# A planner's chains without a gap, four more pairs by seven products, and h and the fourth output chunk handled in another order

## The chip, the cores and the metric

The kernel runs on one core of one Trainium2 chip. The metric is the device time of one execution in microseconds (us), lower is better. The kernel before takes 1148.96 us, the median of 3 runs (1148.46 to 1150.25).

## The reference

One layer of a hybrid encoder on 256 tokens of width 2048, in 32-bit floats. Cut to what matters:

```python
hn = rms_norm(h, g_mix_pre)                       # (256, 2048)
u = hn @ w_in                                     # 2048 x 5120: q, k, v, x, gate
attn = neighborhood_attention(q, k, v, rpb)       # 8 heads of 128
rec = rglru_bidirectional(x, ...) * gelu(gate)    # width 1024
mixed = concat(rms_norm(attn, g_attn_out), rms_norm(rec, g_rec_out)) @ w_out   # 2048 x 2048
h = h + rms_norm(mixed, g_mix_post)
fn = rms_norm(h, g_ffn_pre)
ff = (silu(fn @ w_ffn_gate) * (fn @ w_ffn_up)) @ w_ffn_down    # 2048 x 5632 twice, 5632 x 2048
h = h + rms_norm(ff, g_ffn_post)
gate = sigmoid(rms_norm(h, g_ple_pre) @ w_ple_gate)            # 2048 x 2048
h = h + rms_norm(gate * (p @ w_ple_proj), g_ple_post)          # p is (256, 256)
```

## The kernel before, in words

**Products.** The tokens are two tiles of 128. Every product is done in three matmuls, because both sides are split in a high part that the matmul takes as it is and a low part, the rest: high by high, high by low, low by high (`products`, L565 to L567; `times3`, L577 to L579). A matmul is 128 x 128 by 128 x 512. The weights come from memory as tiles of 128 x 2 x 512 (512 KB, two blocks of 128 rows each, a pair "k") into a few raw slots `wr` (`load_stream`, L491, all on SP's queue). ACT casts a tile to its high part `wh` (`hi_stream`, L516), DVE subtracts it to get the low part `wl` (`lo_stream`, L526). There are 6 slots for the split tiles, one more from the FFN on, and one more that is lent.

**Seven products in place of eight.** The FFN's gate and up projection, the down projection and the last gate work on a pair of output chunks by a `Group`. For each pair k of row blocks a unit is either plain ("p": 8 block products, 24 matmuls) or by the Strassen-Winograd scheme ("s": 7 block products, 21 matmuls, `seven`). An "s" unit needs sums of weight blocks (`sum_stream`: four subtractions of 128 x 512 on DVE, L546 and L550, into slots `ts`), and its second raw tile is split by half only: the first tile, half the second and the two sums are split, three and a half tiles in place of two. It needs sums of activation blocks too (`act_sums`, L1574 and the split of L312 and L314, once per pair k and left side). The matmuls of "s" units that have no plain partner gather in four banks p1, p5, p6 and p7; after the last "s" unit of a group, `Seven.early` (L1695 to L1708) combines them, and `late` adds the result to the other four banks. Which units are "s" is written by hand: `KINDS` (L89) has one digit for each of the 11 groups of gate and up, "2" or "3" being their number (group 0 uses `FIRST` with two), and `DOWN` (L66) lists the units of the down projection by part. Part 3 has one group for chunks 0 and 1, and plain chunks 2 and 3 after it.

**From the gate to the down projection.** `Gated.late` multiplies gate and up, turns the blocks (a DVE transpose, and a round trip through memory by DMA, `turn`, L348 and L356) and splits them into `mid0`, `mid1` or `mid2`, the left side of the down projection of the three parts: groups 0 to 3, 4 to 7 and 8 to 10. Where the down projection has an "s" unit, `act_sums` follows.

**The mixing layer's output.** `w_out` has four chunks of 512 columns, each with an attention half (`A_KS`, four pairs) and a recurrent half (`R_KS`). They have different scales per token (`r_attn` and `r_rec`, the reciprocals of roots `rt_attn` and `rt_rec`), so for each chunk `attn_part` (L1625) writes the attention half times `r_attn` to `mg` on ACT, and `rec_part` (L1639) adds the recurrent half times `r_rec` on DVE. Then `summed` takes the sum of squares (`squares`, L1423, ACT) and multiplies by the gain (L1415, DVE). The order is attention 0, attention 1, recurrent 0, recurrent 1, then attention and recurrent of 2, and of 3. Then PE has two chunks of the small embedding product while `next_norm` sums the squares (L1438), takes the root, waits for all four chunks' gains, and computes h (L1459), which PE transposes (L332) and ACT and DVE split (L318, L320) as the left side of the FFN.

**Lending.** h is needed again only after the FFN. When the squares of h (L1470) are planned, `lend_h` writes h to memory (L1483, `kept`, 2 x 1024 KB), and its two buffers serve as one split slot (`lent_w`) and two raw slots (`lent_r`) until `give_back` loads h again. The gain's buffer is lent as the two slots for sums (`lent_t`).

**The order of the work.** The kernel builds its instruction queues with a `Plan` that runs while the program is written. Each task is a generator that yields its next operation's engine and cost: DVE 0.08 + 0.00104 us per element, ACT 0.12 + 0.00082, a matmul 0.2267. The plan keeps a clock per engine, starts the task with the earliest start plus its due time ("late": URGENT, SOON, LATE, ...), and writes its instructions at that place of the queues. After an operation the task is ready again 0.15 us (`SEM`) after its end. PE's products are in fixed order; transposes and other small matmuls go between them when the plan holds them ready. Nothing of the plan's time is on the chip: each engine runs its queue in order and waits by semaphores.

Of the kernel before, what the change touches and what calls it, by code (L numbers as in the profile page):

```python
# [10 lines left out]
F32 = mybir.dt.float32  # L11
# [5 lines left out]
P = 128  # L17
# [41 lines left out]
SM_BUFS = 4  # L59
LATE = 0.6  # L60
MM = 0.2267
# [3 lines left out]
TURN_LATE = -6.0  # L65
DOWN = (("p2 p6 s0 p8 p10 s4 s12 p14", "p2 p6 s0 p10 s4 p8 s12 p14"), ("p2 p6 s0 p8 p10 s4 s12 p14", "p2 p6 s0 p10 s4 p8 s12 p14"), ("p2 p4 s0 p6 p8 p10",))  # L66
URGENT = -3.0
SOON = -0.5
TURNS = 1
# [14 lines left out]
LATE_SUMS = 0.0  # L84
SEED = 0.0
LATE_EVAC = 0.0
# [21 lines left out]
class Plan:  # L108
# [10 lines left out]
    LATENCY = 2.0  # L119
    MARGIN = 0.4  # L120

    def __init__(self, **slots):
# [129 lines left out]
def layer(ctx: ExitStack, tc: tile.TileContext, a: dict, out: bass.AP):  # L252
# [772 lines left out]

    r_of = {n: const.tile([P, NT], F32, name=f"r_{n}") for n in ("attn", "rec")}
    ev_r = {n: Event() for n in r_of}

    def token_rstd(ss, n):
# [7 lines left out]
        tmp = const.tile([P, NT], F32, name=f"rt_{n}")  # L1037
        yield act(NT, SQRT, give="sm")
# [250 lines left out]
    def open_p2():  # L1289
        for e in mixT.ev + list(ev_r.values()):  # L1290
            plan.reach(e)
        p1_ctx.close()
        rs = ctx.enter_context(tc.tile_pool(name="rs", bufs=1))
        t2["pool"] = rs
        t2["mg"] = rs.tile([P, NT, D], F32, name="mg")
# [59 lines left out]
    class Sub:  # L1355


        def __init__(self, name, gain, gname):
# [7 lines left out]
        def chunk(self, c, ch, add=False):  # L1366
# [7 lines left out]
            for t in range(NT):  # L1374
# [5 lines left out]
                plan.add(self.squares(c, t, src, squared[t]), plan.now, URGENT if c == 3 else 0.0)  # L1380
            for t in range(NT):
                src = mg[:, t, sl] if add else ch.accs[t]
                if early:
                    yield act(N)
                    nc.scalar.copy(mg[:, t, sl], src)
                else:
                    if add:
                        yield squared[t]
                    yield dve(N)
                    nc.vector.tensor_tensor(  # L1390
                        out=mg[:, t, sl], in0=src, in1=t2["gain"][:, sl], op=ALU.mult
                    )
            for e in squared:
# [26 lines left out]
        def squares(self, c, t, src, ev):  # L1420
            yield act(N)
            junk = t2["pool"].tile([P, N], F32, tag="junk", name="junk", bufs=1)
            nc.scalar.activation(junk, src, AF.Square, accum_out=self.ss[:, t, c : c + 1])  # L1423
            done(ev)
            done(self.sums[c][t])
# [4 lines left out]
    def next_norm(sub, nxt, rstd, ev_rstd, g_next):  # L1430
# [171 lines left out]

    mix = Sub("mix", "g_mix_post", "g_ffn_pre")
    hF = Act()
    rstd_f, ev_rf = small("rstd_f"), Event()
# [489 lines left out]
```

## Time and profile before

| | |
|---|---|
| median of 3 runs | 1148.96 us |
| the profiled execution | 1149.72 us, span 1147.9 us |
| PE busy, matmuls | 1134.6 us, 5135 |
| DVE busy | 973.4 us |
| ACT busy | 722.5 us |
| DMA | 257.69 MB, mean 224 GB/s |
| granted TensorE clock | 0.998 |

PE is the matmul engine (PEld its weight loads), DVE the vector engine, ACT the scalar engine, SP the one whose queue issues nearly all DMAs. A row of waits reads: who waited, at which line, for whom; total us, times, longest. A row of a window has its length, then busy us and the number of instructions of PE, PEld, DVE, ACT and POOL, the granted clock, the DMA engines' busy share and GB/s. A row of a timeline has the start, the duration, the engine, the line, the operation, out<-in, the shapes and a count; in brackets how long the engine sat idle before it and what ended that. Durations of neighbours overlap, so the cost of one among many is read from start to start. A matmul of 512 columns shows 0.39 us and starts 0.227 us after the one before.

### The profile page before, as it was taken

How to read it: one execution, taken by the hardware profiler on the slowest of the kernel's cores; microseconds unless marked ns; L12 is line 12 of the kernel's file. 1: busy time of each engine (PE TensorE's matmuls, PEld its weight loads, DVE VectorE, ACT ScalarE, POOL GpSimd, SP SyncE). 2: the span in 40 equal slices, each digit the busy share in tenths (PEclk: the TensorE clock that was granted, in tenths of full speed). 3: DMA queues.
4: the chain of work that ended last, by engine and by line, in shares of the span. 5: the costliest groups of instructions: out<-in, count | busy, mean ns of one | idle time of the engine just before them, and what ended most of it. 6: DMA issues, size and time to landing. Idle time of an engine off the chain costs nothing.

```text
span 1147.9 us, 14639 instructions
## 1 busy us (share of the span) xinstructions
PE 1134.6 (99%) x5135; PEld 941.4 (82%) x5135; DVE 973.4 (85%) x1280; ACT 722.5 (63%) x975; POOL 1.6 (0%) x13
## 2 busy tenths in 40 slices
PE   9999999999999999999999999999999999999996
PEld 7888888888888788888888888888888888888885
DVE  6777887877659899889989889999987999877996
ACT  7775888686558755555565455565655547566863
POOL 0000000000000000000000000000000000000000
PEclk9999999999999999999999999999999999999999
DMA  9876768557865778586576776767776757985561
GB/s 354 290 241 203 251 194 240 167 181 261 321 196 174 256 242 264 197 254 227 194 235 195 222 218 187 224 231 214 223 244 202 220 186 245 295 305 185 173 194 73
DMA packets 83594, 257.69 MB, mean 224 GB/s; under 512 B 9024, under 2 KB 24768, under 8 KB 82112
## 3 DMA queue, kind: packets, MB, share of 16 engines
q1 hardware_dynamic: 83376, 256.68, 69.5%
q8 instruction: 40, 0.66, 0.2%
q14 instruction: 34, 0.28, 0.1%
q10 hardware_dynamic: 144, 0.08, 0.0%
HBM read 242.04 MB, written 14.68 MB: 224 GB/s over the span
## 4 chain that ended last, share of the span: by engine, by line
PE 96%; DMA 1%; ACT 1%; DVE 1%; issue 0%; SPq 0%; DVEq 0%; ACTq 0%
PE c L566 14%; PE c L567 14%; PE c L565 14%; PE acc L565 12%; PE acc L566 11%; PE acc L567 11%; PE p L579 3%; PE p L578 3%; PE p L577 3%; PE c L579 2%; PE c L578 2%; PE c L577 2%; DMA kept<-h 1%; PE tr L332 0%; DVE h L1459 0%; ACT junk L1470 0%
## 5 line engine op out<-in xcount | busy, mean ns | idle before, releaser
L526 DVE TENSOR_TENSOR wl<-wr,wh 128x1024 fp32r<-128x1024 f32 (+1 forms) x318 | 368.6, 1171 | 78.3 <-ACT wh L516 77.0
L516 ACT CAST wh<-wr 128x1024 fp32r<-128x1024 f32 (+1 forms) x318 | 317.5, 1011 | 153.4 <-PE c L567 55.5
L565 PE MATMUL c<-wh,hT_mix_hi 128*128 128x512 f32 x428 | 167.0, 390 | 0.6 <-ACT hT_mix_hi L318 0.6
L567 PE MATMUL c<-wh,hT_mix_lo 128*128 128x512 f32 x428 | 166.6, 389 | 0.0
L566 PE MATMUL c<-wl,hT_mix_hi 128*128 128x512 f32 x428 | 166.5, 389 | 0.0
L516 ACT CAST wh<-lent_t 128x1024 fp32r<-128x1024 f32 x71 | 74.1, 1053 | 111.2 <-DVE lent_t L550 76.1
L565 PE MATMUL acc<-wh,hT_hi 128*128 128x512 f32 x320 | 126.5, 395 | 1.2 <-ACT wh L516 1.2
L566 PE MATMUL acc<-wl,hT_hi 128*128 128x512 f32 x320 | 125.3, 392 | 0.0
L567 PE MATMUL acc<-wh,hT_lo 128*128 128x512 f32 x320 | 125.2, 391 | 0.0
L565 PEld LDWEIGHTS c<-wh,hT_mix_hi 128*128 128x128 f32 x428 | 80.3, 188 | 17.4 <-ACT hT_mix_hi L318 0.9
L567 PEld LDWEIGHTS c<-wh,hT_mix_lo 128*128 128x128 f32 x428 | 80.3, 188 | 16.9 <-DVE hT_mix_lo L320 0.2
L566 PEld LDWEIGHTS c<-wl,hT_mix_hi 128*128 128x128 f32 x428 | 80.4, 188 | 16.5
L526 DVE TENSOR_TENSOR wl<-lent_t,wh 128x1024 fp32r<-128x1024 f32 x71 | 85.1, 1220 | 9.5 <-ACT wh L516 9.3
L516 ACT CAST wh<-lent_r 128x1024 fp32r<-128x1024 f32 (+1 forms) x59 | 57.4, 986 | 29.1 <-PE c L567 20.1
L565 PEld LDWEIGHTS acc<-wh,hT_hi 128*128 128x128 f32 x320 | 60.5, 189 | 13.2 <-ACT wh L516 1.5
L567 PEld LDWEIGHTS acc<-wh,hT_lo 128*128 128x128 f32 x320 | 60.4, 189 | 12.8
L566 PEld LDWEIGHTS acc<-wl,hT_hi 128*128 128x128 f32 x320 | 60.5, 189 | 12.4 <-DVE wl L526 0.4
L526 DVE TENSOR_TENSOR wl<-lent_r,wh 128x1024 fp32r<-128x1024 f32 (+1 forms) x59 | 66.7, 1136 | 3.0 <-ACT wh L516 3.0
L578 PE MATMUL p<-wl,sums_f 128*128 128x512 f32 x75 | 29.3, 390 | 0.0
L579 PE MATMUL p<-wh,sums_f 128*128 128x512 f32 x75 | 29.2, 389 | 0.0
L577 PE MATMUL p<-wh,sums_f 128*128 128x512 f32 x75 | 29.2, 389 | 0.0
L516 ACT CAST lent_w<-wr 128x1024 fp32r<-128x1024 f32 (+1 forms) x23 | 21.1, 916 | 11.0 <-PE c L567 10.0
(508 smaller groups left out, 2335.4 us busy)
## 6 DMA issues: line engine op xcount, KB each, us to landing
wr<-in_w_in SPq DMA_DIRECT2D x77, 512.0 KB, 4.7
wr<-in_w_ffn_down SPq DMA_DIRECT2D x70, 512.0 KB, 4.8
wr<-in_w_ffn_gate SPq DMA_DIRECT2D x64, 512.0 KB, 4.5
wr<-in_w_ffn_up SPq DMA_DIRECT2D x64, 512.0 KB, 4.3
wr<-in_w_out SPq DMA_DIRECT2D x32, 512.0 KB, 4.7
lent_r<-in_w_ffn_up SPq DMA_DIRECT2D x24, 512.0 KB, 4.2
lent_r<-in_w_ffn_gate SPq DMA_DIRECT2D x24, 512.0 KB, 4.3
wr<-in_w_ple_gate SPq DMA_DIRECT2D x24, 512.0 KB, 4.2
```

What stands on the lines that cost most here:

```text
L516: nc.scalar.copy(his[i][:, j, :], raws[i][:, j, :])
L526: nc.vector.tensor_tensor(out=los[i][:, j, :], in0=raws[i][:, j, :], in1=f32(his[i][:, j, :]), op=ALU.subtract,)
L565: nc.tensor.matmul(accs[t], hi[t], wh[:, j, :], start=st, stop=False, **mm)
L566: nc.tensor.matmul(accs[t], hi[t], wl[:, j, :], start=False, stop=False, **mm)
L567: nc.tensor.matmul(accs[t], lo[t], wh[:, j, :], start=False, stop=sp, **mm)
L577: nc.tensor.matmul(o, lh, wh, start=start, stop=False, **mm)
L578: nc.tensor.matmul(o, lh, wl, start=False, stop=False, **mm)
L579: nc.tensor.matmul(o, ll, wh, start=False, stop=stop, **mm)
```

## The change

- `KINDS`: groups 2, 3 and 8 have three "s" units in place of two. `DOWN`: in part 3, pair 8 is an "s" unit.
- The planner's `SAME`: if a task's next operation is on the engine of the last one (DVE or ACT), it is ready at the end of that, with no 0.15 us between. `LATE` goes from 0.6 to 0.5 and `SOON` from -0.5 to -0.25.
- Chunk 3 of `w_out`: its attention half runs before the recurrent half of chunk 2. ACT writes it to PSUM times the ratio r_attn / r_rec (a new operation of DVE makes the ratio), and the recurrent half is accumulated on top of it. The squares read PSUM with the scale r_rec, and one DVE operation per tile multiplies by r_rec and the gain. The addition is gone.
- `Sub.chunk` lets the gain of chunk 3 wait for the squares, in the FFN's norm too.
- `next_norm` waits for the gain of each chunk just ahead of h's operations on it; the gain's buffer is lent, or loaded again, at chunk 3.
- h is written to memory in two halves of its columns (`write_h`), each planned when h has them; lending waits for both.
- `SQUARED` is empty for both norms, so the new branch in `squares` that would use DVE is not taken. `R_SEED` is -2.0, the other new constants are 0.

```diff
-LATE = 0.6
+LATE = 0.5
-DOWN = (..., ("p2 p4 s0 p6 p8 p10",))
+DOWN = (..., ("p2 p4 s0 p6 s8 p10",))
-SOON = -0.5
+SOON = -0.25
-KINDS = tuple({"2": "ppppspsp", "3": "ppspspsp"}[f] for f in "32223233233")
+KINDS = tuple({"2": "ppppspsp", "3": "ppspspsp"}[f] for f in "32333233333")
...
         self._next(task, end + self.LATENCY if eng == "dma" else None)
+        if eng in self.SAME and task.op and not isinstance(task.op, Event) and task.op[0] == eng:
+            task.ready = end
...
+    def ratio():
+        for n in ("attn", "rec"):
+            yield ev_r[n]
+        yield dve(NT)
+        nc.vector.tensor_tensor(out=r_of["ratio"], in0=r_of["attn"], in1=rt_of["rec"], op=ALU.mult)
+        done(ev_r["ratio"])
...
             for t in range(NT):
+                if c == 3:
+                    yield squared[t]
...
+                    if self.scale is None or c < 3:
                         nc.vector.tensor_tensor(out=mg[:, t, sl], in0=src, in1=t2["gain"][:, sl], op=ALU.mult)
+                    else:
+                        nc.vector.scalar_tensor_tensor(
+                            out=mg[:, t, sl], in0=src, scalar=self.scale[:, t : t + 1],
+                            in1=t2["gain"][:, sl], op0=ALU.mult, op1=ALU.mult,
+                        )
...
-            nc.scalar.activation(junk, src, AF.Square, accum_out=self.ss[:, t, c : c + 1])
+                nc.scalar.activation(
+                    junk, src, AF.Square, scale=scale, accum_out=self.ss[:, t, c : c + 1]
+                )
...
-        for e in sub.chunks:
-            yield e
-        if n == "mix":
-            lend_gain()
-            plan.add(gain_back(), plan.now)
-        else:
-            plan.add(next_gain(g_next, plan.now), plan.now)
...
             if c > 1:
                 yield nxt.ev[4 * c - 8]
+            yield sub.chunks[c]
+            if c == 3 and n == "mix":
+                lend_gain()
+                plan.add(gain_back(), plan.now)
+            elif c == 3:
+                plan.add(next_gain(g_next, plan.now), plan.now)
...
+            if n == "mix" and c % 2:
+                plan.add(write_h(h, c - 1), plan.now, H_WRITE)
...
+    def write_h(h, c):
+        sl = slice(c * N, (c + 2) * N)
+        yield dma(1024)
+        if not c:
+            t2["kept"] = [kept.tile([P, D], F32, name=f"kept{t}") for t in range(NT)]
+        for t in range(NT):
+            nc.sync.dma_start(t2["kept"][t][:, sl], h[t][:, sl])
+        ev_kept[c // 2].t = plan.now + LANDED
...
     def lend_h(h):
-        t2["kept"] = [kept.tile([P, D], F32, name=f"kept{t}") for t in range(NT)]
-        for t in range(NT):
-            yield dma(1024)
-            nc.sync.dma_start(t2["kept"][t], h[t])
-        there = Event()
-        there.t = plan.now + LANDED
-        yield there
+        for e in ev_kept:
+            yield e
...
+    mix.scale = r_of["rec"]
...
-    for c, rec in ((0, 0), (1, 0), (0, 1), (1, 1), (2, 0), (2, 1), (3, 0), (3, 1)):
-        late = URGENT if c == 3 else 0.0
-        if rec:
-            seg(Chunk(rec_part(c), None, late, "acc" if c else "sm"), "w_out", c * N, mixT, R_KS)
+    r3 = Chunk(sub_post(mix, 3, False, after_mix), None, URGENT, "sm")
+    r3.seeded = Event()
+
+    def a3_post(ch):
+        yield ev_r["ratio"]
+        r3.accs, r3.at = [], 0.0
+        for t in range(NT):
+            yield act(N, take="sm")
+            acc = ps.tile([P, N], F32, tag="sm", name=f"acc{t}", bufs=ACC_BUFS)
+            r3.accs.append(acc)
+            nc.scalar.activation(acc, ch.accs[t], AF.Copy, scale=r_of["ratio"][:, t : t + 1])
+        release(ch)
+        done(r3.seeded)
+
+    for c, rec in ((0, 0), (1, 0), (0, 1), (1, 1), (2, 0), (3, 0), (2, 1), (3, 1)):
+        late = R_SEED if c == 3 else 0.0
+        if c == 3:
+            seg(r3 if rec else Chunk(a3_post, None, R_SEED), "w_out", c * N, mixT, R_KS if rec else A_KS)
+        elif rec:
+            seg(Chunk(rec_part(c), None, late, "acc" if c == 1 else "sm"), "w_out", c * N, mixT, R_KS)
```

More of the change, by code (lines that the diff above doesn't have):

```diff
@@ L85 @@
 SEED = 0.0
+SAME = ("dve", "act")
+SQUARED = {"mix": (), "ffn": ()}
+R_SEED = -2.0
+GAINED = 0.0
+H_WRITE = 0.0
 LATE_EVAC = 0.0
@@ L120 @@
     MARGIN = 0.4
+    SAME = SAME
     def __init__(self, **slots):
@@ L1026, in layer @@
     r_of = {n: const.tile([P, NT], F32, name=f"r_{n}") for n in ("attn", "rec")}
+    r_of["ratio"] = const.tile([P, NT], F32, name="r_ratio")
     ev_r = {n: Event() for n in r_of}
+    rt_of = {}
+    def ratio():
[4 more added lines that the diff above has]
+        done(ev_r["ratio"])
     def token_rstd(ss, n):
@@ L1289, in open_p2 @@
     def open_p2():
-        for e in mixT.ev + list(ev_r.values()):
+        for e in mixT.ev + [ev_r["attn"], ev_r["rec"]]:
             plan.reach(e)
@@ L1293, in open_p2 @@
         rs = ctx.enter_context(tc.tile_pool(name="rs", bufs=1))
+        plan.add(ratio(), plan.clk["pe"])
         t2["pool"] = rs
@@ L1389, in chunk @@
                     yield dve(N)
-                    nc.vector.tensor_tensor(
-                        out=mg[:, t, sl], in0=src, in1=t2["gain"][:, sl], op=ALU.mult
-                    )
+                    if self.scale is None or c < 3:
+                        nc.vector.tensor_tensor(
+                            out=mg[:, t, sl], in0=src, in1=t2["gain"][:, sl], op=ALU.mult
+                        )
[4 more added lines that the diff above has]
+                        )
             for e in squared:
@@ L1420, in squares @@
         def squares(self, c, t, src, ev):
-            yield act(N)
-            junk = t2["pool"].tile([P, N], F32, tag="junk", name="junk", bufs=1)
-            nc.scalar.activation(junk, src, AF.Square, accum_out=self.ss[:, t, c : c + 1])
+            scale = 1.0 if self.scale is None or c < 3 else self.scale[:, t : t + 1]
+            if c == 3 and t in SQUARED[self.name]:
+                yield dve(N)
+                nc.vector.scalar_tensor_tensor(
+                    out=t2["mg"][:, t, c * N : (c + 1) * N], in0=src, scalar=scale, in1=src,
+                    op0=ALU.mult, op1=ALU.mult, accum_out=self.ss[:, t, c : c + 1],
+                )
+                if self.scale is not None:
+                    yield dve(1)
+                    nc.vector.tensor_tensor(
+                        out=self.ss[:, t, c : c + 1], in0=self.ss[:, t, c : c + 1], in1=scale, op=ALU.mult
+                    )
+            else:
+                yield act(N)
+                junk = t2["pool"].tile([P, N], F32, tag="junk", name="junk", bufs=1)
+                nc.scalar.activation(
+                    junk, src, AF.Square, scale=scale, accum_out=self.ss[:, t, c : c + 1]
+                )
             done(ev)
```

6 lines of the change are left out of this document (4 added, 2 removed).

## The prediction

> **What bounds the kernel now.** I read the page first, then who waited for whom on PE, then the table by stage, and then the timeline of the two places where PE waits.
>
> ```profile
> span 1147.9 us, 14639 instructions
> PE 1134.6 (99%) x5135; PEld 941.4 (82%) x5135; DVE 973.4 (85%) x1280; ACT 722.5 (63%) x975; POOL 1.6 (0%) x13
> PE 96%; DMA 1%; ACT 1%; DVE 1%; issue 0%; SPq 0%; DVEq 0%; ACTq 0%
> ```
>
> PE is busy 99% of the span and carries 96% of the chain that ended last. So a product less is time less, as long as no other engine makes PE wait. These are PE's waits, all of them:
>
> ```profile
> PE acc L565 <- ACT wh L516: 1.2, 1, 1.2
> PE warm L819 <- DVE xn L822: 1.0, 1, 1.0
> PE c L566 <- DVE lent_w L526: 1.0, 1, 1.0
> PE c L565 <- ACT hT_mix_hi L318: 0.6, 1, 0.6
> ```
>
> The first two are the start of the program and nothing in the change touches them. The last two, 1.04 us and 0.64 us in the timeline, are where PE waits in the middle. The stages of the FFN (the shorter windows are single groups; "x" counts instructions):
>
> ```profile
> 347.00:604.10 257.10, 255.42 (x1139) 210.91 (x1138) 235.18 (x305) 152.24 (x191) 0.00 (x0) 1.00 0.71 229
> 394.70:436.80 42.10, 42.10 (x187) 34.89 (x186) 39.70 (x49) 24.68 (x27) 0.00 (x0) 1.00 0.77 249
> 562.60:604.10 41.50, 41.50 (x184) 34.35 (x183) 37.72 (x45) 22.52 (x24) 0.00 (x0) 1.00 0.70 215
> 853.70:1010.80 157.10, 157.10 (x694) 129.97 (x693) 140.36 (x164) 87.00 (x97) 0.00 (x0) 1.00 0.73 232
> 937.30:978.80 41.50, 41.50 (x185) 34.35 (x184) 40.38 (x47) 24.69 (x31) 0.00 (x0) 1.00 0.72 225
> ```
>
> The columns are PE, PEld, DVE and ACT busy. After 394.7 us PE is busy in the whole of each window. DVE is next: 91.5% from 347.0 to 604.1 us (235.18 of 257.10), 89.3% from 853.7 to 1010.8 us, and 97.3% in the group of 937.3 us, which has three pairs by seven products and in which PE is still busy throughout. ACT (59% and 55% of the two long windows) is not near a limit.
>
> **The products.** A group of eight pairs takes 8 x 24 matmuls, less 3 for each pair by seven products (21 in place of 24): 183 with three such pairs. The window of 562.6 us is one, 41.50 / 183 = 0.227 us each. The change turns one pair more in each of the groups 2, 3 and 8 of the FFN, and one in the third part of the down projection: 4 x 3 x 0.227 = 2.72 us of PE less. All four lie where PE is the path. Whether the four are made isn't in doubt: they are written in KINDS and DOWN, not chosen by the planner.
>
> **What the four cost on DVE.** A pair by seven products has four sum operations (L546, L550) on DVE, and its weights are split as three and a half tiles in place of two.
>
> ```profile
> 433.24 0.69 DVE L1703 TENSOR_TENSOR u_hi<-p,mid 128x512 f32<-128x512 f32 x1
> 433.97 0.69 DVE L1705 TENSOR_TENSOR mid<-p,mid 128x512 f32<-128x512 f32 x1
> 434.58 1.22 DVE L526 TENSOR_TENSOR wl<-lent_r,wh 128x1024 fp32r<-128x1024 f32 x1
> ...
> 442.46 0.68 DVE L546 TENSOR_TENSOR lent_t<-lent_r,wr 128x512 f32<-128x512 f32 x1
> 443.06 1.22 DVE L526 TENSOR_TENSOR lent_w<-wr,lent_w 128x1024 fp32r<-128x1024 f32 x1
> 444.20 0.69 DVE L550 TENSOR_TENSOR lent_t<-lent_r 128x512 f32<-128x512 f32 x1
> ```
>
> From start to start a sum takes 0.60 us and a split 1.14 us. So a pair adds 4 x 0.60 + 1.5 x 1.14 = 4.11 us of DVE work, and 1.5 casts on ACT, which has room. I cost this at nothing, for it lies beside PE: from 347.0 to 604.1 us DVE's work goes to 235.18 + 2 x 4.11 = 243.4 us, and PE's time, without the two waits and 6 matmuls, to 254.1 us: 95.8%. From 853.7 to 1010.8 us two pairs and one more set of activation sums (1.7 us, rows below) make 150.3 of 155.7 us, 96.5%. Both are under the 97.3% that the group at 937.3 us bore, and seven or eight split tiles stand ready between DVE and PE. If that cover is gone, each us of DVE over PE's time is one of PE's: the second rival.
>
> **The end of the mixing layer.** Chunk 3 now starts from the attention part in PSUM, so the addition before the squares goes. The order at the turn to the FFN was:
>
> ```profile
> 340.72 1.40 DVE L1639 SCALAR_TENSOR_TENSOR mg<-acc,r_rec,mg 128x512 f32<-128x512 f32 x2
> ...
> 342.17 0.63 ACT L1423 ACTIVATE junk<-mg 128x512 f32<-128x512 f32 x1
> ...
> 347.42 0.33 SPq L491 DMA_DIRECT2D wr<-in_w_ffn_up  x1
> 348.13 0.50 PE L565 MATMUL c<-wh,hT_mix_hi 128*128 128x512 f32 x1 [0.64 <-ACT hT_mix_hi L318]
> ...
> 360.93 0.33 SPq L491 DMA_DIRECT2D wr<-in_w_ffn_gate  x1
> ```
>
> The addition (L1639) began at 340.72 us, when the layer's last products ended, and the squares at 342.17; from PSUM they can begin when the product is there, about 1 us earlier. PE has the embedding's 24 matmuls and h's transposes in between, and then waits. All that follows (sum, root, h, transposes) moves with it, and by waiting for each chunk's own gain instead of all four, h can begin before chunk 3 is multiplied. 0.64 us of wait behind 1 us of chain: I take it as gone. The rest costs nothing: the two scaled copies into PSUM (L1625's two before, the same size) have the 48 matmuls of the chunk between, 10.9 us, as cover; the ratio is one operation of two elements.
>
> **h's writes.** They were issued after the last square of h, and the next weights could go into h's buffers only when they had landed:
>
> ```profile
> 355.30 0.40 DVE h L1459
> ...
> 365.09 10.91 DMA kept<-h
> 376.13 3.78 DMA lent_r<-in_w_ffn_up
> 381.81 0.50 PE L566 MATMUL c<-lent_w,hT_mix_hi 128*128 128x512 f32 x1 [1.04 <-DVE lent_w L526]
> ```
>
> (The last line is PE's timeline, the others the chain.) It ends in PE's wait of 1.04 us. The change issues each half of the columns once h has it. h's last operation ended at 355.7 us and will end about 1 us sooner; if the second half takes the whole 10.91 us, which both halves took before, it has landed by 365.6 us. The squares of h were at their last when the writes were issued, so the first load can go at about 366 us in place of 376. The wait of 1.04 us goes. What is late next is the sum and the split of the same weights, with some 9 us in hand. The cost: on SP the writes wait for h's vector operations, and weight loads stand behind them; between the loads at 347.42 and 360.93 us (rows above) SP had none to issue, so this is free; if that cover were gone, a load would be late by the wait of the write in front of it, 1 to 2 us, against the 9 us won.
>
> **The one place where I see a new wait.** In the third part of the down projection pair 8 is by seven products, and its activations come from group 10 just before: through a round trip by DMA, a split, and now four sums and a split of these.
>
> ```profile
> 996.86 1.05 ACT L312 CAST mid2h<-turned 128x1024 fp32r<-128x1024 f32 x1 [0.36 <-DMA turned<-via]
> 997.86 1.22 DVE L526 TENSOR_TENSOR wl<-wr,wh 128x1024 fp32r<-128x1024 f32 x1
> 999.00 1.22 DVE L314 TENSOR_TENSOR mid2l<-turned,mid2h 128x1024 fp32r<-128x1024 f32 x1
> 999.87 0.39 PE L565 MATMUL c<-wh,mid2h 128*128 128x512 f32 x1
> ...
> 1070.80 0.28 DVE L1574 TENSOR_TENSOR s<-v 128x128 f32<-128x128 f32 x1
> 1071.90 0.62 ACT L312 CAST sums_p<-s 128x512 fp32r<-128x512 f32 x1
> 1072.87 0.68 DVE L314 TENSOR_TENSOR sums_p<-s,sums_p 128x512 fp32r<-128x512 f32 x1
> ```
>
> Before, the block was ready at 1000.1 us and PE took it from 999.87: just in time. The sums take 2.7 us more (1070.80 to 1073.5; 1.7 of it, 1070.80 to 1071.90 and 0.60, is DVE's at most), so 1002.8 us. PE needs them six matmuls later (two products of the block itself come first) and their low half two matmuls after that: 999.87 + 8 x 0.227 = 1001.7 us. In the old order that is a wait of 1.1 us. One more weight split ahead on DVE makes it 2.2. If DVE turns to the block when ACT has it (997.9, not 999.0), it is 0; and the combining of the p products (L1698 to L1708), which ran in these microseconds, now comes after pair 8, so DVE has less ahead of it here. I take 0.6 us, between 0 and the old order's 1.1, and keep 0 and 2.2 for the range.
>
> **The planner.** It only sets the order in each queue; none of its times reaches the chip. It charged 0.76 us for a step of 512 elements in a chain on DVE, its 0.61 and 0.15 of signal; now 0.61. In the rows above the step from L1703 to L1705 takes 0.73 us from start to start, and L1705 to an operation that doesn't need it 0.61. So its old figure was 0.03 too long and the new one is 0.12 too short: the gap does not vanish on the chip. Some seven steps of this kind a group (L1698 to L1708, the activation sums) are 0.8 us by which the plan may be early. I cost it at nothing, with a bound of 1.2 us either way, the largest wait that PE now has. The same goes for the shifted due times (LATE, SOON), which can reorder the attention stage too. The Trainium skill, VectorE: DVE Perf Modes, section The DRAIN you can't avoid, says that a chain of vector operations takes the same with a signal after each as with one at the end. By that rule the new figure would be right, the plan exact, and this term nothing; the rows show 0.12 us for the dependent step, so I keep the bound.
>
> **The sum**, against the profiled execution's 1149.72 us (span 1147.9 and 1.8 around it): 1149.72 - 2.72 - 1.04 - 0.64 + 0.6 = 1145.92. That execution lay 0.76 us above the median of the three runs, 1148.96; so 1145.2 us. A difference of 0.2%, 2.3 us, is about what a measurement of this kernel can tell from no change.
>
> **Rival 1: new waits eat half of it.** Pair 8 waits 2.2 us (1.6 more than I took) and the reordered queues cost PE the 1.2 us of the bound: 1148.0 us. For it: the block was just in time before, and PE waits nowhere else, so a reordering can only add. Against it: the planner knows each of these events and orders by them.
>
> **Rival 2: DVE becomes the bound, and the kernel is slower.** The place is the groups 2 and 3, and 8 to 10 with the down projection after them. DVE's work there is 243.4 + 150.3 = 393.7 us against 254.1 + 155.7 = 409.8 us of PE. If over such stretches DVE cannot be kept busy more than the 94.3% of the window at 394.7 us (39.70 of 42.10), it needs 417.5 us: 7.7 us more, and 1145.2 - 0.6 + 7.7 = 1152.3 us. All 4.4 us of gain are gone when DVE's share stops at 95.0% (393.7 / 414.2). For it: no long window shows over 92%, and DVE waits for ACT in chains. Against it: PE never asked for more than that there, and a single group had 97.3%. The Trainium skill, Perfetto Trace Analysis, section Identifying the Most-Contended Engine, holds matmul busy time a bad measure and DVE's occupancy a fair one; by that rule DVE's 85% counts for more than PE's 99% and speaks for this rival. The trace speaks against the rule here: matmul starts stand 0.227 us apart and PE has no wait in these stages.
>
> **Rival 3: everything is hidden**, pair 8 too: 1144.6 us. It belongs to the same side as the forecast.
>
> **How the numbers follow.** Forecast with rival 3: 0.66, all of it under 1146.7 us, so faster. Rival 1: 0.23, within 0.2%. Rival 2: 0.11, slower. The likeliest value is 1145.2. The range goes from 1144.2 (rival 3, and 0.4 for the reordering turning out well) to 1149.0 (rival 1, with 1 us of rival 2); beyond it I leave about 0.15.
>
> **What would show it.** Right: 12 matmuls fewer on PE; no PE wait on lent_w near 381 us nor on hT_mix_hi near 347; the first load into lent_r issued near 366 us, not 376; squares of chunk 3 read from PSUM about 1 us earlier; four more DVE sums per pair and PE still full from 395 to 1010 us. Wrong: PE waits on wl or wh in the groups 2, 3 and 8 to 10 (rival 2), on the sums of the third part near 1000 us or in the attention stage (rival 1). The forecast is wrong if the PE waits after 20 us sum to over 2 us.

## The result, and the profile after

The kernel after takes 1159.33 us, the median of 4 runs (1158.41 to 1163.4). The kernel before, run beside it, takes 1149.28. The ratio is 1.0094, with a 95% interval of 1.0079 to 1.0109: slower by 10 us, where 1145.2 was forecast and 1149.0 was the end of the range. The profiled execution took 1158.41 us. In two of the runs below one slow execution is left out of the median: 2330.87 us in the run with `SAME` from the mixing layer on, and 1262.4 us in the run with a gap of 0, of which it is the only profile.

The page of the kernel after:

```profile
span 1156.6 us, 14709 instructions
PE 1135.1 (98%) x5123; PEld 940.4 (81%) x5123; DVE 995.0 (86%) x1308; ACT 725.0 (63%) x983; POOL 1.6 (0%) x13
PE 83%; DVE 7%; DMA 4%; ACT 4%; issue 2%; SPq 0%; DVEq 0%; ACTq 0%
```

PE has the 12 matmuls less, but its busy time did not fall (1134.6 before), and its share of the chain went from 96% to 83%. Who waited for whom on PE:

```profile
PE pg L377 <- ACT gh L320: 3.9, 2, 2.1
PE pg L379 <- DVE gl L322: 3.4, 3, 1.9
PE acc L573 <- ACT wh L524: 1.4, 1, 1.4
PE warm L827 <- DVE xn L830: 1.0, 1, 1.0
PE sc L378 <- DVE kl L322: 0.8, 1, 0.8
...
PE c L585 <- ACT sums_m L320: 0.4, 1, 0.4
PE c L587 <- DVE sums_m L322: 0.4, 1, 0.4
```

The waits on lent_w and hT_mix_hi are gone. The new ones are 7.3 us on gh and gl, the split gate weights of the recurrent part, and 0.8 us on kl, all in the attention stage (that is, all work ahead of the mixing layer's products). The first product of `w_out` starts at 255.3 us before and at 267.5 us after. The table by stage, cut at these two times, first of before, then of after:

```profile
20.00:255.30 235.30, 235.30 (x1149) 198.21 (x1148) 183.06 (x275) 183.93 (x285) 0.00 (x0) 1.00 0.72 230
```

```profile
20.00:267.50 247.50, 239.04 (x1149) 199.69 (x1148) 191.38 (x285) 185.89 (x291) 0.00 (x0) 0.99 0.71 222
394.70:521.20 126.50, 126.50 (x559) 104.75 (x559) 122.65 (x146) 75.04 (x84) 0.00 (x0) 1.00 0.73 234
853.70:1010.80 157.10, 156.72 (x691) 129.18 (x690) 148.16 (x179) 90.25 (x102) 0.00 (x0) 1.00 0.70 228
```

The same 1149 matmuls take 12.2 us longer: 8.46 us PE is idle (247.50 less 239.04), and 3.74 us it works longer (239.04 less 235.30), at a lower granted clock. In the FFN PE is full, as forecast. So the whole loss lies ahead of 267.5 us, and behind it the kernel after is 3.5 us quicker (12.2 late there, 8.7 in the span).

**How the loss comes about.** This is ACT's timeline of the kernel after, ahead of the third pair of gates:

```profile
147.16 0.46 ACT L1250 ACTIVATE attnT<-po,vec 128x256 f32<-128x256 f32 x1
151.14 1.05 ACT L524 CAST wh<-wr 128x1024 fp32r<-128x1024 f32 x1 [3.52 <-DMA wr<-in_w_in]
152.10 0.61 ACT L320 CAST at_hi<-attnT 128x512 fp32r<-128x512 f32 x1
154.99 1.05 ACT L524 CAST wh<-wr 128x1024 fp32r<-128x1024 f32 x1 [2.28 <-DMA wr<-in_w_in]
155.94 2.33 ACT L913 COPY xp<-ev 128x256 f32<-128x256 f32 x4
...
162.21 0.62 ACT L320 CAST xch<-xc 128x512 fp32r<-128x512 f32 x1 [2.04 <-DVE xc L955]
...
163.89 1.04 ACT L320 CAST gh<-av 128x1024 fp32r<-128x1024 f32 x1
```

ACT stands 3.52 and 2.28 us at casts of weights that have not landed. Behind them in its queue are the copies xp, from which the recurrent part goes on: the plan had them at 141.56 us of its own clock, as written out while it runs, and the chip did them at 155.94. The cast gh was planned for 149.03 and came at 163.89, 14.9 us late. In the kernel before the same cast was planned for 150.15 and came at 153.89:

```profile
146.72 2.34 ACT L905 COPY xp<-ev 128x256 f32<-128x256 f32 x4
...
153.89 1.04 ACT L312 CAST gh<-av 128x1024 fp32r<-128x1024 f32 x1
```

PE's queue was written by the plan's clock. So PE met the gate products before gh was there, with the products of `w_in` queued behind them. PE's timeline of the kernel after:

```profile
164.98 0.39 PE L377 MATMUL pg<-xch,gh 128*128 128x256 f32 x1 [2.07 <-ACT gh L320]
...
167.37 0.39 PE L379 MATMUL pg<-xch,gl 128*128 128x256 f32 x1 [1.88 <-DVE gl L322]
...
169.37 0.63 PE L573 MATMUL acc<-wh,hT_hi 128*128 128x512 f32 x1
169.80 0.63 PE L574 MATMUL acc<-wl,hT_hi 128*128 128x512 f32 x1
```

After the two waits the products start 0.43 us apart in place of 0.227. From 167.59 to 171.35 us the products take some 1.5 us more than at their usual spacing, which is a part of the 3.74 us; the rest was not located row by row.

### The profile page after: what moved, and what is told of

It is laid out like the page before. It is cut to its first block, busy times and chain, and to the rows that moved or that the text cites. A ratio compares the mean times of both kernels' runs of the same rounds, so it can differ in the third digit from the quotient of the medians.

```text
span 1156.6 us, 14709 instructions
## 1 busy us (share of the span) xinstructions
PE 1135.1 (98%) x5123; PEld 940.4 (81%) x5123; DVE 995.0 (86%) x1308; ACT 725.0 (63%) x983; POOL 1.6 (0%) x13
## 4 chain that ended last, share of the span: by engine, by line
PE 83%; DVE 7%; DMA 4%; ACT 4%; issue 2%; SPq 0%; DVEq 0%; ACTq 0%
PE c L575 13%; PE c L574 13%; PE c L573 13%; PE acc L574 8%; PE acc L573 8%; PE acc L575 8%; PE p L586 4%; PE p L587 4%; PE p L585 4%; PE c L587 3%; PE c L586 3%; PE c L585 3%; DVE wl L534 2%; DMA wr<-in_w_in 2%; ACT wh L524 1%
## 5 line engine op out<-in xcount | busy, mean ns | idle before, releaser
L534 DVE TENSOR_TENSOR wl<-wr,wh 128x1024 fp32r<-128x1024 f32 (+1 forms) x319 | 363.1, 1166 | 73.7 <-ACT wh L524 72.8
L524 ACT CAST wh<-lent_t 128x1024 fp32r<-128x1024 f32 x78 | 81.8, 1053 | 166.7 <-DVE lent_t L558 147.5
L573 PE MATMUL c<-wh,hT_mix_hi 128*128 128x512 f32 x408 | 159.1, 390 | 0.0
L575 PE MATMUL c<-wh,hT_mix_lo 128*128 128x512 f32 x408 | 158.8, 389 | 0.0
L574 PE MATMUL c<-wl,hT_mix_hi 128*128 128x512 f32 x408 | 158.7, 389 | 0.0
L534 DVE TENSOR_TENSOR wl<-lent_t,wh 128x1024 fp32r<-128x1024 f32 x78 | 94.6, 1218 | 11.2 <-ACT wh L524 10.2
L575 PEld LDWEIGHTS c<-wh,hT_mix_lo 128*128 128x128 f32 x408 | 76.6, 188 | 15.9
L574 PEld LDWEIGHTS c<-wl,hT_mix_hi 128*128 128x128 f32 x408 | 76.6, 188 | 15.8
L585 PE MATMUL p<-wh,sums_f 128*128 128x512 f32 x83 | 32.3, 389 | 0.0
L587 PE MATMUL p<-wh,sums_f 128*128 128x512 f32 x83 | 32.3, 389 | 0.0
L573 PE MATMUL c<-wh,mid0h 128*128 128x512 f32 x72 | 28.0, 389 | 0.0
```

The lines of the kernel that those rows point to most:

```text
L524: nc.scalar.copy(his[i][:, j, :], raws[i][:, j, :])
L534: nc.vector.tensor_tensor(out=los[i][:, j, :], in0=raws[i][:, j, :], in1=f32(his[i][:, j, :]), op=ALU.subtract,)
L573: nc.tensor.matmul(accs[t], hi[t], wh[:, j, :], start=st, stop=False, **mm)
L574: nc.tensor.matmul(accs[t], hi[t], wl[:, j, :], start=False, stop=False, **mm)
L575: nc.tensor.matmul(accs[t], lo[t], wh[:, j, :], start=False, stop=sp, **mm)
L585: nc.tensor.matmul(o, lh, wh, start=start, stop=False, **mm)
```

## The experiments

**The theories.** A: without the 0.15 us between dependent operations the plan runs ahead of the chip, and PE's queue meets gate and score products too early. The rivals at first were the shifted due times, and the other edits (pairs, h, fourth chunk).

B came up after the first four runs, from a closer reading of the planner. In `_run`, the call `_next` takes the task to its next operation; where it passes an event whose time is known already (a weight load that will land), it moves the task's ready time to that. The two new lines stand behind this call and set `task.ready = end`. So they drop not only the 0.15 us, but the landing too. That happens at 38 places of the kernel after between 6 and 265 us of the plan's clock, by up to 2.96 us, 37 of them on ACT and 36 of these casts of weights (the expectations below say 37 in all).

**The planner as before, all other edits in.**

```diff
-LATE = 0.5
+LATE = 0.6
-SOON = -0.25
+SOON = -0.5
-SAME = ("dve", "act")
+SAME = ()
```

> The changed kernel with the planner as before (no SAME, LATE 0.6, SOON -0.5); the four pairs, chunk 3, h's writes and the norms stay changed. Theory A (the planner's order of the attention stage costs 12.4 us, all the rest of the change gains some 3.7): no wait of PE on the gate weights, 1145 to 1146 us. Rival B (the four pairs or the other edits cost too, hidden so far): 1147 us or more.

1146.89 us, ratio 0.9983 (0.9974 to 0.9993). This lies between what the two sides expected. The other edits are a gain of 2.25 us against 1149.14 in the same comparison, so the loss is the planner's.

**Parts of the planner alone.** The kernel before with SAME alone, the kernel before with the due times alone, and the kernel after with `SAME = ()`:

> The kernel before with SAME alone. Theory A1 (SAME makes the plan's clock run ahead of the chip, so that PE is given the gate products too early): PE waits on gh and gl, 1159 to 1162 us, and the first product of the FFN 10 to 13 us later than before. Rival A2 (the shifted due times do it): within 1 us of 1149.

> The kernel before with LATE 0.5 and SOON -0.25 alone. Theory A1 (SAME does it): within 2 us of 1149. Rival A2 (the due times do it): 1159 to 1162 us with PE waiting on gh and gl.

> The changed kernel without SAME, the due times changed (LATE 0.5, SOON -0.25). Theory A1: the attention stage is as before, 1145 to 1147 us. Rival A2: 1157 us or more. If SAME and the due times only do it together: near 1146 here, and runs 2 and 3 both near 1149.

SAME alone: 1173.6 us, 1.0208 (1.0172 to 1.0245). Due times alone: 1153.37 us, 1.0043 (1.0030 to 1.0056). After without SAME: 1149.71 us, 1.0008 (0.9999 to 1.0017). None of the three lies where a theory had put it. SAME is the larger part, 24.5 us on the kernel before and 9.6 in the kernel after (1159.33 less 1149.71), and the due times cost something too; in both profiles with the due times and without SAME PE waits 1.7 us on rec_lo, at the recurrent half of `w_out`.

**The two halves of SAME.** Landings kept and the gap gone, then the gap kept and the landings thrown away:

```diff
-        if eng in self.SAME and ... and task.op[0] == eng:
+        if eng in self.SAME and ... and task.op[0] == eng and task.ready <= end + self.SEM:
             task.ready = end
```

> The kernel after, but where a task passes over an event whose time the plan knows already (a weight load's landing above all), the next operation on the same engine still waits for that time; only the 0.15 us between dependent operations stay dropped. Its plan issues the four gate loads at 56.5, 92.4, 142.2 and 176.9 us of its own clock, the last 6 us earlier than in the kernel after. Theory A (the dropped 0.15 us per step makes the plan of the attention stage run ahead of the chip): as the kernel after or worse, 1157 to 1163 us, PE waits on gh and gl of 5 us and more. Theory B (the new line also throws away known landings, in 37 places from 6 to 265 us by up to 2.96 us, so that casts stand in ACT's queue before their weights are there and the gates' work waits behind them): as without SAME, 1148 to 1151 us, ACT waits on loads of w_in back from 29.3 us to about 15.5.

```diff
-        if eng in self.SAME and ... and task.op[0] == eng:
-            task.ready = end
+        if eng in self.SAME and ... and task.op[0] == eng and task.ready > end + self.SEM:
+            task.ready = end + self.SEM
```

> The other half: the kernel after with the 0.15 us kept everywhere, but a known landing still thrown away where the next operation is on the same engine. Theory A: as without SAME, 1148.5 to 1151 us, no PE wait on gh or gl over 0.5 us. Theory B: most of the loss stays, 1156 to 1161 us, ACT waits on w_in's loads near 29 us.

1152.64 us, 1.0031 (1.0020 to 1.0041), and 1153.4 us, 1.0031 (1.0021 to 1.0041). Both times lie between what the theories expected, so neither is right alone. From 1149.71 the gap alone adds 2.9, the landings alone 3.7, both 9.6. With the landings kept PE waits less for the gates, but for kh and kl:

```profile
PE sc L377 <- ACT kh L320: 2.0, 1, 2.0
...
PE sc L378 <- DVE kl L322: 1.1, 1, 1.1
PE pg L379 <- DVE gl L322: 1.1, 2, 0.8
```

**SAME for DVE alone** (`SAME = ("dve",)`):

> The kernel after with SAME for DVE alone. Of the 37 dropped landings 36 are on ACT, so Theory B expects 1148.5 to 1151 us. Theory A expects a loss in the share of DVE's chains (27 steps of the decay and the convolution's steps, in all some 60 steps of 0.15 us before the last gates): 1153 to 1160 us, with PE waits on gh and gl.

1159.59 us, 1.0089 (1.0076 to 1.0102), outside what Theory B allowed, and not where Theory A put it: the first product of `w_out` came at 257.7 us, and the loss was one wait of 8.1 us at the start of the FFN, taken up below.

**The pairs alone, and the edits to h and the fourth chunk alone**, each on the kernel before:

> The kernel before with KINDS and DOWN of the kernel after alone (four more pairs by seven products). By the terms of the prediction, 12 matmuls of 0.227 us less and a wait of 0.6 us on pair 8's sums: 2.1 us less, 1147.0 us, ratio 0.998, the waits on lent_w (1.0) and hT_mix_hi (0.6) still there. If the added DVE work costs PE something, 1148.5 us or more with waits on wl or the sums.

> The kernel before with the two edits to h and to the fourth chunk alone: the planner and the pairs as before. By the prediction's terms the waits of 1.04 and 0.64 us go: 1147.5 us, ratio 0.9985. If the chain behind is only late somewhere else, 1149.2 us. With the pairs on top it was 1146.9 us, and the pairs alone gave no gain (1.0013), so if the pairs pay only with the earlier writes of h, this one is at 1147.5 to 1149 us.

The pairs: 1150.96 us, 1.0013 (1.0004 to 1.0022), no gain. In the profile of that run PE waits on split weights in group 2, which has a new pair, and at pair 8:

```profile
460.33 0.50 PE L578 MATMUL p<-lent_w,sums_f 128*128 128x512 f32 x1 [0.39 <-DVE lent_w L526]
462.22 0.50 PE L566 MATMUL c<-wl,hT_mix_hi 128*128 128x512 f32 x1 [0.23 <-DVE wl L526]
1002.15 0.50 PE L578 MATMUL p<-wl,sums_m 128*128 128x512 f32 x1 [0.39 <-DVE wl L526]
```

That profile is of the quickest execution, 1147.82 us, so these 1.0 us do not explain a median that is 3.1 us higher.

The edits to h and the chunk: 1148.32 us, 0.9992 (0.9984 to 1.0001), a gain of 1.0 us in the median, with an interval that reaches no gain. With the pairs on top it was 1146.89, in another comparison. So the pairs bring some 1.4 us there, with intervals that overlap, and nothing without the earlier writes of h. The traces, read stage by stage below, give the same 1.4.

**A wider margin.** `MARGIN = 4.0` in the kernel after.

> The kernel after with MARGIN 4.0 in place of 0.4: a small matmul of PE (gates, scores, transposes) is put into PE's queue only when the plan has held its inputs ready for 4 us. If the loss of 12.2 us ahead of the mixing layer's products is PE standing at gate and score products that the plan held ready too early, the waits on gh, gl and kl (8.1 us in the kernel after) fall to under 2 us and the first product of w_out comes at 256 to 260 us in place of 267.5; the time is then 1150 to 1153 us, if the later gates don't make a wait of their own behind. If the loss is of another kind (other work late), the first product of w_out stays at 264 us or later and the time at 1157 us or more.

1156.74 us, 1.0062 (1.0047 to 1.0078), between the two cases. No wait on gh, gl or kl is left, but others took their place, and `w_out` began at 263.2 us:

```profile
PE acc L574 <- DVE wl L534: 3.2, 3, 1.5
PE po L377 <- ACT r L974: 1.6, 1, 1.6
```

PE standing at small products is thus one part only: with them out of the way PE waits for the weights' low parts (wl), so ACT's and DVE's queues, which the margin does not touch, are late too.

**SAME from the mixing layer on.** Empty until `open_p2`, then as in the kernel after.

> The kernel after with SAME empty until the mixing layer's products are planned and on from there. If the loss lies in the attention stage alone, the time is that of the kernel after without SAME, 1149 to 1151 us, with the first product of w_out at 254 to 257 us. If SAME costs in the FFN as well, 1152 us or more.

1150.28 us, 1.0007 (0.9997 to 1.0016); `w_out` began at 255.0 us. Without SAME it was 1149.71: from the mixing layer on SAME neither costs nor gains within 1 us.

**The size of the gap.** All with the old due times and landings kept; the line reads `task.ready = end + 0.12`, and then 0, 0.06 and 0.20. The last of the five is 0.12 with landings thrown away, as in the kernel after.

> The kernel after with the old due times, known landings kept, and 0.12 us between dependent operations on one engine in place of none: the gap that the trace shows for a 512-element step on DVE. If the size of the gap is what hurts, the plan is 0.03 us a step from the old one and the time 1146.5 to 1149 us, with no wait on gh and gl over 0.5 us. If any reordering of this stage costs, 1151 us or more.

> As the run with 0.12 us (old due times, landings kept), but with a gap of 0 between dependent operations on one engine. If the gap's size is the cause: 1152 to 1158 us, first product of w_out after 260 us, waits on gh, gl, kh or kl of 3 us and more. If the due times were what hurt: 1145 to 1148 us.

> As the run with 0.12 us, with a gap of 0.06. A dose that counts puts it between, 1147 to 1154 us; if every order other than the old one is a draw of its own, it may lie anywhere from 1145 to 1158 us.

> As the run with 0.12 us, with a gap of 0.20: the plan is now too late for DVE's chains by some 0.05 to 0.1 us a step. If only a plan that is ahead of the chip makes PE wait: 1145 to 1149 us, without waits on gh and gl over 0.5 us. If any shift hurts: 1150 us or more.

> As the run with 0.12 us, but known landings are thrown away as in the kernel after. Alone on the new due times and 0.15 us, throwing them away cost 3.7 us in the median (1153.4 against 1149.71). If that cost is its own: 1148 to 1150 us. If it is nothing once the gap is right: 1145 to 1147 us.

All runs with the other edits in that differ by these three settings; the kernel before lay between 1148.84 and 1149.89 us beside them, so two of these times compare to some 1 us. The last two columns are from the profile: the first product of `w_out`, and ACT's waits on the loads of `w_in` from 20 us on.

| due times | landings | gap, us | time, us | ratio | w_out at | ACT waits |
|---|---|---|---|---|---|---|
| old | kept | 0.20 | 1171.86 | 1.0194 (1.0178 to 1.0210) | 255.7 | 13.8 |
| old | kept | 0.15 | 1146.89 | 0.9983 (0.9974 to 0.9993) | 255.1 | 18.2 |
| old | kept | 0.12 | 1145.54 | 0.9966 (0.9954 to 0.9979) | 255.8 | 16.9 |
| old | kept | 0.06 | 1156.99 | 1.0062 (1.0048 to 1.0076) | 257.0 | 16.0 |
| old | kept | 0 | 1150.72 | 1.0008 (0.9997 to 1.0019) | not read | not read |
| old | thrown | 0.12 | 1162.37 | 1.0114 (1.0098 to 1.0130) | 264.8 | 29.9 |
| new | kept | 0.15 | 1149.71 | 1.0008 (0.9999 to 1.0017) | 255.1 | 16.5 |
| new | kept | 0 | 1152.64 | 1.0031 (1.0020 to 1.0041) | 263.0 | 20.3 |
| new | thrown | 0.15 | 1153.40 | 1.0031 (1.0021 to 1.0041) | 254.4 | 17.2 |
| new | thrown | 0 (after) | 1159.33 | 1.0094 (1.0079 to 1.0109) | 267.5 | 26.9 |

Theory A falls as a dose: 0, 0.06, 0.12, 0.15 and 0.20 give 1150.7, 1157.0, 1145.5, 1146.9 and 1171.9. A plan that is too late (0.20) is the worst, so being ahead of the chip is not the only harm; 0.12 came out 1 us better than expected. What is left of A is that 0 is slower than 0.15 with either due times, by 2.9 and 3.8 us. Theory B holds in sign: landings thrown away cost in each of the three pairs that differ in nothing else, 3.7, 6.7 and 16.8 us; the last gave 1162.4 us, where 1150 at most was expected. The 0.12 run with them thrown away looks like the kernel after:

```profile
ACT wh L524 <- DMA wr<-in_w_in: 29.9, 18, 3.5
```

```profile
PE acc L573 <- ACT rec_hi L326: 2.7, 1, 2.7
PE sc L377 <- ACT kh L320: 2.4, 1, 2.4
```

**One place behind the doses.** The runs of 0.06, of 0.20 and of DVE alone have one wait in common. Of the 0.06 run, ACT's timeline and PE's:

```profile
357.44 0.64 ACT L1513 ACTIVATE junk<-h 128x512 f32<-128x512 f32 x1
...
362.73 0.63 ACT L1513 ACTIVATE junk<-h 128x512 f32<-128x512 f32 x1
...
363.88 0.57 ACT L1640 COPY ple<-acc 128x512 f32<-128x512 f32 x1
...
364.50 0.80 PE L573 MATMUL c<-wh,hT_mix_hi 128*128 128x512 f32 x1 [8.54 <-ACT ple L1640]
```

The copy of the embedding product frees a bank of PSUM that the FFN's first products need. In this order it stands behind eight squares of h, 6 us of ACT. Its due time alone is edited. The queues ahead of it stay as they were; behind it the plan orders other work anew as well:

```diff
-        seg(Chunk(ple_post(c)), "w_ple_proj", ...
+        seg(Chunk(ple_post(c), None, URGENT), "w_ple_proj", ...
```

> The run with a gap of 0.06 us, with the copies of the embedding product given the due time URGENT, so that they stand ahead of the squares of h in ACT's queue. If the 8.5 us wait is a matter of that place alone: no wait on ple over 1 us and 1147.5 to 1150 us. If the plan with 0.06 is late elsewhere too: 1152 us or more.

1145.71 us, 0.9978 (0.9968 to 0.9987), better than expected: 11.3 us less by the due time of these copies. The trace accounts for nearly all of it. Behind the wait of 8.54 us twelve products start 0.43 us apart, until 369.73 us; they take 2.5 us more than at 0.227, and 8.5 and 2.5 make 11.0:

```profile
365.09 0.63 PE L574 MATMUL c<-wl,hT_mix_hi 128*128 128x512 f32 x1
...
369.73 0.39 PE L573 MATMUL c<-wh,hT_mix_hi 128*128 128x512 f32 x1
```

Both copies now come before the squares, as they do in the 0.12 run:

```profile
349.12 0.58 ACT L1640 COPY ple<-acc 128x512 f32<-128x512 f32 x1
349.95 0.60 ACT L1640 COPY ple<-acc 128x512 f32<-128x512 f32 x1
```

So gaps from 0.06 to 0.15 lie within 1.4 us, 1145.5 to 1146.9, once that place is right. In the 0.20 run the same wait has 7.8 us, and one on the recurrent part's squares has 7.6:

```profile
PE c L573 <- ACT ple L1640: 7.8, 1, 7.8
PE pb_rec L1051 <- DVE ssr L1068: 7.6, 1, 7.6
```

**The due times with 0.12.**

> The run with 0.12 us and landings kept, with LATE and SOON as in the kernel after. With the 0.15 us plan the new due times cost 2.8 us (1149.71 against 1146.89), with a wait of 1.7 us on rec_lo: the same here gives 1147.5 to 1149.5 us. If every order is a draw of its own, anything from 1144 to 1160 us.

1151.78 us, 1.0024 (1.0014 to 1.0035): 6.2 us more than with the old ones. PE waits 3.0 us on rec_lo, the place of the 1.7 us seen with 0.15:

```profile
PE acc L575 <- DVE rec_lo L328: 3.0, 1, 3.0
```

With the due times alone on the kernel before (4.2), with 0.15 (2.8) and with 0 (1.9, 1152.64 against 1150.72) that is four pairs, all to the slower side.

**The best of all** are the change with a milder planner: old due times, landings kept, and 0.12 us (0.9966), or 0.06 us with the copy first (0.9978). Both are quicker than the kernel before and the kernel after, and lie within 0.6 us of the 1145.2 that the prediction made for a harmless planner.

## Why the prediction was wrong

**The step that failed** is the planner's: "I cost it at nothing, with a bound of 1.2 us either way, the largest wait that PE now has." It measures 12.4 us (1159.33 less 1146.89). Going from the run with the old plan to the kernel after one edit at a time, it is 2.8 for the due times, 2.9 for the gap and 6.7 for the landings. In another order of the edits the parts differ (the landings cost 3.7 with a gap of 0.15), so they are no prices of their own. Three things were wrong in it.

- The code was taken at its description. The prediction spoke of a gap of 0.12 us that does not vanish; that the two lines throw the landings away stands in the diff, behind the call of `_next`, and was overlooked. It then argued that "the planner knows each of these events and orders by them", which SAME had just undone.
- The bound was no bound. The waits that PE had came from one order; another order has other waits, up to 8.5 us in one place. What stands behind an operation in its engine's queue sets the price (the copies xp and the cast gh on ACT, the products of `w_in` on PE), not the microseconds of the misjudged step.
- It counted some seven steps of a group of the FFN. The loss was in the attention stage, which it named in half a sentence.

The Trainium skill, VectorE: DVE Perf Modes, section The DRAIN you can't avoid, was set against this term: by its rule a plan without gaps would be exact. The trace of the kernel before does not bear that out, though the prediction read it from the wrong pair of rows. L1705 does not need the result of L1703, it overwrites what L1703 reads. The step that needs the last result is from L1698 to L1703, at 433.24 us, and takes 0.72 us, against 0.61 where the next operation does not need the last:

```profile
432.52 0.68 DVE L1698 TENSOR_TENSOR mid<-p,mid 128x512 f32<-128x512 f32 x1
```

The times of the runs agree, but do not measure the step: with landings kept, 0 gave 1152.64 us against 1149.71 with 0.15 on the new due times, and 1150.72 against 1145.54 with 0.12 on the old.

**The other terms came nearly right.** From the first product of `w_out` to the end the kernel after is 3.5 us quicker (889.1 us against 892.6, profiled executions), where the prediction's terms but the planner's give 3.8. Where they come from shows in the starts of PE's first product on each left side: h for the FFN, `mid0` (the down projection's first part), `mid2` (its third) and h for the last gate.

| first product on | before | h and chunk 3 alone | these and the pairs, old planner | after |
|---|---|---|---|---|
| h, FFN | 348.13 | 349.30 | 347.98 | 360.40 |
| `mid0` | 521.15 | 520.95 | 518.26 | 530.31 |
| `mid2` | 978.79 | 978.59 | 975.22 | 987.27 |
| h, last gate | 1050.67 | 1050.31 | 1047.56 | 1059.82 |
| (PE's last) | 1138.13 | 1137.80 | 1135.05 | 1146.90 |

**The products.** The 12 matmuls went, as forecast. The pairs of groups 2 and 3 lie between h and `mid0`, that of group 8 between `mid0` and `mid2`. With the old planner they shorten the two stretches from 171.65 to 170.28 us and from 457.64 to 456.96, together by 2.05 us, which is nine matmuls: they pay in full. The term that was mis-sized is the wait at pair 8. From `mid2` to the last gate the time grows from 71.72 to 72.34 us with three matmuls (0.68 us) fewer, so pair 8 costs 1.3 us where 0.6 was taken, and all four pairs bring 1.4. With the old planner PE waits there for a weight split, the case that the prediction kept for its range, and the products around the wait start further apart, by some 0.5 us:

```profile
1001.11 0.50 PE L586 MATMUL p<-wl,sums_m 128*128 128x512 f32 x1 [0.76 <-DVE wl L534]
```

In the kernel after it is the sums, 0.75 us (0.39 and 0.36, the rows of sums_m above). From `mid2` to PE's last matmul it takes 159.63 us against 159.34 before, again with three matmuls fewer: 1.0 us. Without the earlier writes of h the pairs of groups 2 and 3 pay nothing: from h to `mid0` the run with the pairs alone takes 173.28 us, before it was 173.02. That the lent buffers come too late for them there is argued from its waits, not shown. In the kernel after PE is full from 394.7 to 1010 us, at 97.0% (122.65 of 126.50) and 94.3% (148.16 of 157.10) of DVE.

**The writes of h** did what was forecast. The first load into lent_r goes at 376.79 us, which without the 12.3 us that the FFN begins later is 364.5; forecast were 366. The wait of 1.04 us is gone.

```profile
376.79 0.33 SPq L499 DMA_DIRECT2D lent_r<-in_w_ffn_up  x1
```

**The fourth chunk.** The wait on hT_mix_hi is gone from the list. Counted from the first product of `w_out`, the squares start 1.6 us earlier (352.83 us here, 342.17 before) and h's operations 1.0 us earlier, as forecast. Yet from that product of `w_out` to the first of the FFN it is 92.9 us, and was 92.8. The place of the wait is filled with work: PE has 16 of h's transposes ahead of the FFN's first product, and had 8, first before, then after:

```profile
346.46 1.03 PE L332 MATMUL tr<-ident,h 128*128 128x128 f32 x8
```

```profile
357.34 0.60 PE L340 MATMUL tr<-ident,h 128*128 128x128 f32 x4
...
359.17 1.48 PE L340 MATMUL tr<-ident,h 128*128 128x128 f32 x12
```

So the gain shows behind it: from h to `mid0` the kernel after takes 169.91 us against 173.02, 3.1 us less, and six matmuls and the wait of 1.04 us are 2.4 of that. The rest fits the eight transposes that are no longer in this stretch (16 against 24). The two edits together were costed at 1.68 us and measured at 1.0 by themselves, with an interval that reaches no gain at all.

**The rivals.** Rival 1 named the reordered queues and the attention stage, which was the place; its size was ten times too small, and so it ended within 0.2% and not on the slower side. Rival 2, DVE as the bound, is refuted for the kernel after by the full windows; a short wait on wl remains in the run with the old planner (0.76 us above). The slower side should have been a reordered queue.

**What stays open.** Why thrown landings cost 3.7 us in one order and 16.8 in another was not followed operation by operation; with a gap of 0.15 they left `w_out` on time in the profile, which was the quickest of that kernel's executions, and PE waited behind it, at the end of the recurrent part:

```profile
PE pb_rec L1051 <- DVE ssr L1068: 2.2, 1, 2.2
```

Which order a given gap leads to was only seen, not foreseen. Why a gap of 0 is slower, and where the pairs alone lose what they save, was not found.

## What to carry to other kernels

A planner that writes in-order queues turns a small error of its clock into an order, and the order into a wait: so an edit to it gets a run of its own, and its price here was set by what was queued behind, not by the size of the error. When a loss has come, look at the engine ahead of the one that waits: PE stood for gh, but ACT stood for loads, and in another order copies behind eight squares were worth 11 us. When a stage seems to win nothing, count its work too: a wait can go and other work take its place. And read what a new line overwrites, not only what it adds.

## What the runs showed of the hardware

In these traces a wait cost PE more than its own length. After 2.07 and 1.88 us of wait within 5 us, the 512-column products of the kernel after started 0.43 us apart in place of 0.227 until about 171 us. In the 0.06 run, with its wait of 8.54 us, the granted clock of the stage was 0.89:

```profile
347.80:394.70 46.90, 37.43 (x168) 30.53 (x167) 37.35 (x67) 31.31 (x59) 0.00 (x0) 0.89 0.63 210
```

There the slow products behind the wait came to 2.5 us on top of it. The Trainium skill, TensorE: Matmul & The Clock Gate, section Part 1: The HAM clock gate, states half the clock after an idle window of about 3.4 us, and 426.7 ns a product of 512 columns then. The 0.43 us agree in both runs, and the wait of 8.54 us is longer than such a window; but in the kernel after PE had matmuls between the two waits, and neither of them filled one.
